# Making the low halves of a mixer's plain weight blocks on ScalarE and by an adding DMA

## The chip, the cores and the metric

The kernel runs on one core of one Trainium2 chip. The core has TensorE (PE: matrix products), VectorE (DVE), ScalarE (ACT), GpSimd (POOL, used here only to issue DMAs that add to their target) and SyncE (SP, which issues the plain DMAs). Each engine works through its own queue in order; semaphores carry the dependences between them. The metric is the device time of one execution in microseconds, less is better; the time given is the median of the runs.

## The reference

Two layers of a decoder trunk over 512 tokens of width 1024, in float32. Each layer is a half-weighted SwiGLU feed-forward block, a mixer, and a second feed-forward block, all with RMS norms around them:

```
h = rms_norm(x, gn[0])
x = x + 0.5 * rms_norm(swiglu(h, w_ffn1_gate[l], w_ffn1_up[l], w_ffn1_down[l]), gn[1])
h = rms_norm(x, gn[2])
proj = h @ w_in[l]
hq, hf, hi, hg, aq, ak, av, gate_a, gate_b = jnp.split(proj, IN_SPLITS, axis=-1)
y_hg = hgrn2_mixer(hq, hf, hi, hg, lb_all[l], hgrn_head_gain[l]) @ w_branch_hgrn[l]
y_at = swa_sink_attention(aq, ak, av, attn_sinks[l]) @ w_branch_attn[l]
mixed = jax.nn.sigmoid(gate_a) * y_hg + jax.nn.sigmoid(gate_b) * y_at
x = x + rms_norm(mixed @ w_out[l], gn[3])
```

`hgrn2_mixer` is a gated linear recurrence over 4 heads of 128 by 128 state; `swa_sink_attention` is attention with 8 query heads over a window of 128 tokens with a learned sink. A second feed-forward block, built like the first, ends the layer.

## The kernel before

**Products in two halves.** TensorE multiplies in a rounded float32 format (`F32R`). To keep float32 accuracy every operand is split into a high half, the operand rounded, and a low half, what the rounding left. `mm3` (a product helper) then makes three products: high with high, high with low, low with high. Nearly all of TensorE's work goes through `mm`, whose matmul is line 115; transposes are line 122.

**The weight stream.** All weights lie in one array, `wall`, of units of 128 by 1024 float32 (512 KB). The class `Stream` (the object `ws`) brings them in order through three rings of buffers: `W32` = 4 raw buffers (tag `w32`, filled by SP's loads of line 241), and `WS` = 6 buffers each for high (`whi`) and low (`wlo`) halves. `Stream.split` makes one unit ready: ScalarE casts the raw block to the high half (line 321), and the low half is made in one of two ways, by the kind of the item. For the kind "u" VectorE subtracts the high half from the raw block (line 328). For the kinds "v", "a" and "d" ScalarE multiplies the raw block by -1 into the low buffer (line 325), and POOL issues a DMA that adds the raw block to it (line 326). The multiply rounds, so raw minus rounded remains, as in the other way; it reads the raw block alone and does not wait for the cast. A raw buffer is given back when all that read it are done, and only then SP loads the unit four places on. Units are split three ahead of the one in use, as far as the six low and high buffers allow.

**What uses the stream.** A mixer's first 34 units are plain blocks: the projections of two recurrence heads (`quad`), attention's keys, queries and values (`project`), two projections by tokens (`project_tok`), two more heads, and the first gate columns with their branch weights (`branch`). After these come units of the fast matrix products (`gates`, items "a" to "d") and the rows of `w_out`.

**What sets the order.** TensorE's order is written out by hand. The recurrence, the attention and the end of each norm run as coroutines; `Order` counts a time from the matmuls issued and resumes each coroutine after a wait given in the table `WAIT`. The order on the other engines is chosen by a scheduler that knows priorities and an estimate of each step; where `pin` stands, the order of the program is kept.

**The start of a mixer.** The end of the preceding feed-forward block, in `down`, is laced into the mixer's start. `Pre.turn` transposes the normed tokens back (line 122) and ScalarE copies them, scaled by a gain, to the high halves (line 581) while VectorE makes the low halves (line 587). For the last tokens `post` and `norm` run this chain: VectorE adds two partial products (line 708), ScalarE squares with a running sum (line 596), VectorE and ScalarE make the root (lines 601 to 603), VectorE scales (lines 727 and 738), and TensorE transposes the result.

**The recurrence.** Each head's scores are built level by level: `meet` (lines 984 to 988) multiplies decays in on VectorE, ScalarE and VectorE fill a tile `mv` (lines 995 to 1000), TensorE multiplies it, and VectorE copies the product under a mask into place (line 972).

Of the kernel before, what the change touches and what calls it, by code (L numbers as in the profile page):

```python
# [23 lines left out]
H = 4  # L24
# [12 lines left out]
W32, WS, AHEAD, TAIL, PLAIN, FIRST, EARLY, LATE = 4, 6, 3, 4, 4, 7, 4, 8  # L37
# [8 lines left out]
def trunk(ctx: ExitStack, tc: tile.TileContext, xin, wall, gains, lbT, hgain, sinks, c_dist, c_mask, c_ident, out):  # L46
# [328 lines left out]
    ws = Stream()  # L375
# [894 lines left out]
    for l in range(DEPTH):  # L1270
        for n in (0, 2, 4):
            if n == 2:
                ws.plain(2 * H + 6 + 8 + LATE * 3 // 2)
                for _ in range(KT - LATE // 2):
                    ws.gates()
                ws.rows(KT, False)
            else:
                p = FIRST if l + n == 0 else PLAIN
                ws.plain(min(2 * p, 8))
                ws.plain(max(2 * p - 8, 0), "v")  # L1280
                ws.pairs(FT - p)
                ws.rows(FT, True)
# [151 lines left out]
```

## Time and profile before

| | |
|---|---|
| median of 3 runs | 2127.11 us (2126.46 to 2127.39) |
| span of the profiled execution | 2123.9 us |
| its own device time | not listed apart; the runs are 2.6 to 3.5 us above its span |
| TensorE busy | 2110.6 us, 99% of the span |
| VectorE busy | 1573.4 us, 74% |
| ScalarE busy | 1119.0 us, 53% |
| POOL busy | 152.2 us, 7% |
| granted TensorE clock | 0.999 |

In the rows of the profile, a group has the line, the engine, the operation, out<-in by the names of the tiles, the shape and the count; then the busy time in us, the mean time of one in ns, and the idle time of the engine just before them with what ended most of it. A row of the timeline has the start and the length in us, then the same names; a row of several instructions (x4) covers them from the first start to the last end. A row of the waits has who waited for whom, the total in us, the number and the longest. PEld is TensorE's loading of weights, which overlaps its products. The first mixer's plain blocks are used from about 358 to 610 us, the second's from about 1409 to 1660 us.

### The profile page before, as it was taken

To read this page: it belongs to the slowest core of one execution; us is meant where nothing else is said; L and a number is where in the kernel's file an instruction comes from. 1 tells how busy PE (TensorE), PEld (TensorE's weight loads), DVE (VectorE), ACT (ScalarE), POOL (GpSimd) and SP (SyncE) were. 2 spreads that over 40 slices of the span, in tenths; PEclk is the share of its full clock that TensorE was granted. 3 is DMA by queue.
4 is the path that set the end of the run, shared out by engine and by line. 5 is a ranking of instruction groups with operands and counts; after the bars stand their busy time and mean duration, and the time that the engine had idled before them with its cause. 6 is when DMAs were issued, how large, how long until landed. Compare 5 with 4: busy or idle time off the path is not lost.

```text
span 2123.9 us, 34765 instructions
## 1 busy us (share of the span) xinstructions
PE 2110.6 (99%) x13293; PEld 1898.1 (89%) x13293; DVE 1573.4 (74%) x2793; ACT 1119.0 (53%) x1884; POOL 152.2 (7%) x180
## 2 busy tenths in 40 slices
PE   9999999999999999999999999999999999999998
PEld 8899988887888999998899998898778989999987
DVE  5877886768776777789587778767687757777884
ACT  7555555346445555556455556453554545555562
POOL 0011000000000011110001110000000000111000
PEclk9999999999999999999999999999999999999999
DMA  8677663221236357774447775632122463677751
GB/s 251 149 185 182 167 181 118 92 67 64 66 100 208 120 125 176 182 197 123 153 113 177 183 183 141 197 119 80 60 70 60 124 194 110 149 180 182 185 158 51
DMA packets 146870, 298.48 MB, mean 141 GB/s; under 512 B 15664, under 2 KB 73488, under 8 KB 146704
## 3 DMA queue, kind: packets, MB, share of 16 engines
q1 hardware_dynamic: 121216, 228.31, 32.7%
q0 software_dynamic: 25344, 67.91, 18.6%
q8 instruction: 104, 1.70, 0.3%
q14 instruction: 62, 0.51, 0.1%
q10 hardware_dynamic: 144, 0.05, 0.0%
HBM read 213.58 MB, written 14.73 MB: 107 GB/s over the span
## 4 chain that ended last, share of the span: by engine, by line
PE 75%; DVE 7%; ACT 3%; issue 1%; DMA 1%; SPq 0%; ACTq 0%; DVEq 0%
PE acc L115 55%; PE aux L115 19%; DVE s L398 1%; PE aux L122 1%; ACT whi L321 1%; DVE wlo L283 1%; DMA w<-wall 1%; DVE wlo L328 1%; PE acc L122 1%; ACT s L397 1%; DVE tt L265 0%; DVE w L264 0%; DVE s L273 0%; DVE w L274 0%; ACT whi L278 0%
## 5 line engine op out<-in xcount | busy, mean ns | idle before, releaser
L115 PE MATMUL acc<-s,whi 128*128 128x256 f32 (+1 forms) x4968 | 1068.8, 312 | 0.7 <-DVE s L901 0.7
L115 PEld LDWEIGHTS acc<-s,whi 128*128 128x128 f32 x4968 | 810.1, 191 | 48.7 <-issue 3.7
L115 PE MATMUL acc<-s,wlo 128*128 128x256 f32 (+1 forms) x2484 | 770.2, 310 | 0.1
L115 PEld LDWEIGHTS acc<-s,wlo 128*128 128x128 f32 x2484 | 474.1, 191 | 26.0 <-DVE wlo L328 0.4
L321 ACT CAST whi<-w 128x1024 fp32r<-128x1024 f32 (+1 forms) x341 | 316.6, 947 | 242.0 <-PE aux L115 100.2
L115 PE MATMUL acc<-whi,s 128*128 128x512 f32 x1264 | 414.5, 394 | 0.0
L321 ACT CAST whi<-tt 128x1024 fp32r<-128x1024 f32 x154 | 161.4, 1048 | 337.7 <-DVE tt L315 199.5
L328 DVE TENSOR_TENSOR wlo<-w,whi 128x1024 fp32r<-128x1024 f32 (+1 forms) x181 | 218.5, 1216 | 135.3 <-ACT whi L321 131.6
L115 PEld LDWEIGHTS acc<-whi,s 128*128 128x128 f32 x1264 | 237.1, 188 | 55.7 <-issue 3.2
L328 DVE TENSOR_TENSOR wlo<-tt,whi 128x1024 fp32r<-128x1024 f32 x154 | 188.1, 1222 | 101.6 <-ACT whi L321 101.6
L326 POOL DMA_DIRECT2D wlo<-w x160 | 138.2, 865 | 1723.5 <-ACT wlo L325 1363.1
L115 PE MATMUL acc<-wlo,s 128*128 128x512 f32 x632 | 246.7, 390 | 1.2 <-DVE wlo L283 1.2
L115 PE MATMUL aux<-s,whi 128*128 128x256 f32 x1232 | 225.1, 283 | 0.0
L115 PE MATMUL aux<-whi,s 128*128 128x512 f32 x592 | 196.7, 390 | 0.0
L115 PEld LDWEIGHTS aux<-s,whi 128*128 128x128 f32 x1232 | 192.2, 192 | 0.0
L115 PE MATMUL aux<-s,wlo 128*128 128x256 f32 x616 | 174.3, 283 | 0.0
L115 PEld LDWEIGHTS acc<-wlo,s 128*128 128x128 f32 x632 | 118.8, 188 | 25.5 <-DVE wlo L283 2.4
L115 PEld LDWEIGHTS aux<-whi,s 128*128 128x128 f32 x592 | 111.2, 188 | 22.9
L325 ACT ACTIVATE wlo<-w 128x1024 fp32r<-128x1024 f32 (+1 forms) x160 | 129.8, 844 | 0.0
L397 ACT CAST s<-s 128x512 fp32r<-128x512 f32 (+1 forms) x164 | 88.4, 580 | 75.8 <-DVE s L456 72.2
L115 PEld LDWEIGHTS aux<-s,wlo 128*128 128x128 f32 x616 | 118.3, 192 | 0.0
L115 PE MATMUL aux<-wlo,s 128*128 128x512 f32 x296 | 115.2, 389 | 0.0
(182 smaller groups left out, 2189.1 us busy)
## 6 DMA issues: line engine op xcount, KB each, us to landing
w<-wall SPq DMA_DIRECT2D x267, 512.0 KB, 3.7
wlo<-w POOLq DMA_DIRECT2D x83, 512.0 KB, 5.5
w<-wall SPq DMA_DIRECT2D x288, 128.0 KB, 3.4
wlo<-w POOLq DMA_DIRECT2D x77, 256.0 KB, 3.3
x_d<-s SPq DMA_DIRECT2D x48, 256.0 KB, 2.1
s<-x_d SPq DMA_DIRECT2D x48, 256.0 KB, 5.5
w<-wall SPq DMA_DIRECT2D x34, 256.0 KB, 3.2
s<-wall SPq DMA_DIRECT2D x64, 128.0 KB, 3.7
```

The source lines that it names most:

```text
L115: nc.tensor.matmul(o, lhsT, rhs, start=start, stop=stop)
L122: nc.tensor.transpose(o, src, ident)
L283: nc.vector.tensor_tensor(it.lo[:, h[c]], w[c], it.hi[:, h[c]].bitcast(F32), op=ALU.subtract)
L321: i = nc.scalar.copy(it.hi[:, c], w[:, c])
L325: nc.scalar.mul(it.lo[:, c], w[:, c], -1.0)
L326: nc.gpsimd.dma_start(it.lo[:, c].bitcast(F32), w[:, c], accum_op=ALU.add)
L328: nc.vector.tensor_tensor(it.lo[:, c], w[:, c], it.hi[:, c].bitcast(F32), op=ALU.subtract)
L397: nc.scalar.copy(hi, src)
L398: nc.vector.tensor_tensor(lo, src, hi.bitcast(F32), op=ALU.subtract)
```

## The change

The 34 plain units of each mixer were one group of the kind "u". Now the first 4 stay of that kind, and the other 30 are of the kind "v". Their high halves are still cast by ScalarE; their low halves are made by ScalarE's multiply and POOL's adding DMA instead of VectorE's subtraction. Nothing else is edited; the order on VectorE and ScalarE around these steps is chosen anew by the scheduler, that on TensorE and SP stays as it was, instruction for instruction.

```
-                ws.plain(2 * H + 6 + 8 + LATE * 3 // 2)
+                ws.plain(4)
+                ws.plain(2 * H + 2 + 8 + LATE * 3 // 2, "v")
                 for _ in range(KT - LATE // 2):
                     ws.gates()
                 ws.rows(KT, False)
```

With `H` = 4 and `LATE` = 8 the old count is 34 and the new ones are 4 and 30.

## The prediction

> **What bounds the kernel now.** I read the page's busy shares first, then the chain that ended last, then the two mixer stretches as windows, then the waits.
>
> ```profile
> span 2123.9 us, 34765 instructions
> PE 2110.6 (99%) x13293; PEld 1898.1 (89%) x13293; DVE 1573.4 (74%) x2793; ACT 1119.0 (53%) x1884; POOL 152.2 (7%) x180
> PE 75%; DVE 7%; ACT 3%; issue 1%; DMA 1%; SPq 0%; ACTq 0%; DVEq 0%
> ...
> 358.00:610.00 252.00, 250.40 (x1397) 210.32 (x1396) 187.73 (x464) 121.95 (x254) 1.54 (x2) 1.00 0.23 74
> 1409.00:1660.00 251.00, 249.40 (x1393) 209.47 (x1392) 187.32 (x463) 120.95 (x252) 0.94 (x2) 1.00 0.23 73
> ...
> PE aux L115 <- DVE s L972: 3.2, 2, 1.6
> ```
>
> The windows' columns are length, then busy time and count of PE, PEld, DVE, ACT and POOL, the granted clock, the DMA share and GB/s. They are the stretches of the two mixers in which the 34 plain blocks of each are used. TensorE is busy for all but 1.60 us of either (252.00 - 250.40 and 251.00 - 249.40), at full clock, and the wait list gives that idle time an owner: one wait of 1.6 us in each mixer, for VectorE's L972. VectorE is busy for 74% of these stretches and ScalarE for 48%; neither bounds them. The order on TensorE is written out by hand and is the same in the changed kernel, so only two things can move the time: a stop of TensorE that goes, or a new one. All stops that the list shows here are worth 3.2 us, 0.15% of the time, which is the ceiling of a gain. About 0.2% (4.25 us) is what a measurement of this kernel can tell from no change.
>
> **The change, part by part.** For 30 blocks in each of two mixers VectorE's subtraction goes; a negating multiply on ScalarE and an adding DMA from POOL's queue come.
>
> ```profile
> L328 DVE TENSOR_TENSOR wlo<-w,whi 128x1024 fp32r<-128x1024 f32 x179 | 217.2, 1222 | 135.3 <-ACT whi L321 131.6 <-PE aux L115 1.6 <-DMA w<-wall 1.3
> L325 ACT ACTIVATE wlo<-w 128x1024 fp32r<-128x1024 f32 x83 | 86.8, 1046 | 0.0
> L326 POOL DMA_DIRECT2D wlo<-w x160: 862/862/1159, 29.6 to 1989.8; - x160
> DMA to landing us min/median/max: 3.2/4.6/7.5
> ```
>
> VectorE loses 60 x 1.222 = 73.3 us, ScalarE gains 60 x 1.046 = 62.8 us, POOL 60 x 0.862 = 51.7 us. The first mixer's stretch becomes 187.73 - 36.7 = 151.1 us of VectorE and 121.95 + 31.4 = 153.3 us of ScalarE out of 252. All of it lies beside TensorE, so what counts is place, not amount.
>
> *When a block is ready.* The subtraction ended 1.2 us after the cast; the new way takes 1.05 for the multiply, about 0.3 to POOL's start and 4.6 (3.2 to 7.5) to the landing, 6 us and at most 9. The first of the 30 has least room:
>
> ```profile
> 366.16 1.98 ACT L321 CAST whi<-w 128x1024 fp32r<-128x1024 f32 x2
> ...
> 383.70 0.39 PE L115 MATMUL acc<-s,wlo 128*128 128x512 f32 x1
> 395.04 0.39 PE L115 MATMUL acc<-s,wlo 128*128 128x512 f32 x1
> ```
>
> Cast from 366.16, low half read at 383.70: 16.5 us after the cast's end. Its multiply does not need the cast at all, and in the changed order stands well ahead of it. The third, cast at 374.67 (row below), is read at 395.04, 20 us later, and the lead grows from there. Nothing on the path, 0; without that cover it would be some 5 us a block.
>
> *When a raw buffer comes free.* The load four blocks on now waits for the landing instead of the subtraction. The tightest is that of the block cast at 374.67, whose buffer is loaded for the cast at 389.57:
>
> ```profile
> 374.67 1.05 ACT L321 CAST whi<-w 128x1024 fp32r<-128x1024 f32 x1 [3.60 <-PE acc L115]
> 389.57 1.04 ACT L321 CAST whi<-w 128x1024 fp32r<-128x1024 f32 x1 [2.80 <-PE acc L115]
> DMA to landing us min/median/max: 3.3/3.5/5.7
> ...
> 429.86 0.40 PE L115 MATMUL acc<-whi,s 128*128 128x512 f32 x1
> ```
>
> 374.67 + 1.05 + 1.05 + 0.3 + 4.6 + 3.5 = 385.2, before 389.57; with both maxima 390.3, 0.7 late, against a cast whose block TensorE first reads at 429.86. SP's order is unchanged; what queues behind the waiting load there is other loads. 0. POOL's queue holds nothing else in these stretches (two instructions in the first one). 0.
>
> *ScalarE's queue at the start of each mixer.* This is the step on the path. The changed order has the first two multiplies of a mixer (1.046 each, spaced 0.94, as the pair of casts above) between the second and the third scaled copy L581, before the down projection's last tokens are normalised. The rows of before:
>
> ```profile
> 356.85 1.56 ACT L581 ACTIVATE s<-acc,g_sb 128x256 fp32r<-128x256 f32 x4
> 358.29 0.85 ACT L581 ACTIVATE s<-aux,g_sb 128x256 fp32r<-128x256 f32 x2
> 359.00 0.66 ACT L596 ACTIVATE s<-s 128x512 f32<-128x512 f32 x1
> 359.61 0.66 ACT L596 ACTIVATE s<-s 128x512 f32<-128x512 f32 x1
> 360.13 0.23 ACT L596 ACTIVATION_READ_ACCUMULATOR s<-s 128x1 f32 x1
> 361.64 0.29 ACT L602 ACTIVATE rt<-ss,rt 128x1 f32<-128x1 f32 x1 [1.28 <-DVE rt L601]
> ...
> 359.24 0.68 DVE L708 TENSOR_TENSOR s<-aux,s 128x512 f32<-128x512 f32 x1
> 359.83 0.87 DVE L587 SCALAR_TENSOR_TENSOR s<-acc,g_sb,s 128x256 fp32r<-128x256 f32 x2
> 360.62 0.87 DVE L587 SCALAR_TENSOR_TENSOR s<-aux,g_sb,s 128x256 fp32r<-128x256 f32 x2
> 361.40 0.21 DVE L601 TENSOR_SCALAR rt<-ss 128x1 f32<-128x1 f32 x2
> 366.49 0.88 DVE L738 TENSOR_SCALAR s<-s,rt 128x512 f32<-128x512 f32 x2
> ...
> 326.54 11.25 SPq L241 DMA_DIRECT2D w<-wall  x3
> 358.42 0.40 PE L115 MATMUL acc<-s,whi 128*128 128x256 f32 x2
> 367.09 0.60 PE L122 MATMUL acc<-ident,s 128*128 128x128 f32 x4
> ```
>
> The third L581 goes from 357.57 to 359.45, and with it all behind it on ScalarE by 1.88: the last L581 ends at 361.02, the second square's sum is read out at 360.36 + 1.88 = 362.24. ScalarE had been idle for 1.28 before L602, because VectorE was still busy with L587; that idle time takes up most of it. L602 now starts at the sum, 362.25, instead of 361.64: +0.61. From L602 to L738 it is one chain of square, root and scaling, so L738's first half ends at 367.59 instead of 366.98 (second L738 starts 0.40 after the first; each takes 0.49). The second of the four transposes reads it, at 367.20 in before; at the L972 stop TensorE starts 0.14 after VectorE's end, so it starts at 367.73: 0.53 of new idle time in a mixer, 1.06 in both (the second mixer has the same rows around 1408). Bounds: 0, if the chain has more play than its rows show; 1.88 - 0.22 + 0.14 = 1.80 a mixer, 3.6 in all, if nothing is taken up (0.22 is from 366.98 to 367.20). I take 0.53, as the idle row of 1.28 is right there. The multiplies' own waits end in time: the loads that they need were issued by 337.8 (326.54 + 11.25), and TensorE gives back the low buffers with its last reads of the down projection, before it turns to the mixer at 358.42; the second multiply starts at 358.52.
>
> *The L972 stop.* VectorE and TensorE there:
>
> ```profile
> 397.05 1.23 DVE L328 TENSOR_TENSOR wlo<-w,whi 128x1024 fp32r<-128x1024 f32 x1 [2.42 <-ACT whi L321]
> 398.19 0.68 DVE L401 SCALAR_TENSOR_TENSOR s<-acc,s 128x512 fp32r<-128x512 f32 x1
> 400.60 1.29 DVE L972 COPY_PREDICATED s<-mask,aux 128x128 f32<-128x128 int32 x4
> 396.92 0.59 ACT L400 ACTIVATE s<-acc 128x512 fp32r<-128x512 f32 x1
> 401.74 0.89 PE L115 MATMUL aux<-mv,s 128*128 128x192 f32 x4 [1.60 <-DVE s L972]
> ```
>
> The subtraction at 397.05 goes, but L401 behind it needs ScalarE's L400, which ends at 397.51 and itself waits for TensorE. So L401 starts at 397.57, 0.62 earlier, not 1.2. The changed order puts one more masked copy ahead of the one that TensorE waits for, 0.28 by the spacing of the copies in the row of four. Gain 0.34 a mixer, 0.68 in both. Bounds: all of 3.2, or 0 if the reordering eats it.
>
> *ScalarE elsewhere.* At some ten places a mixer a multiply now stands directly ahead of a step that had followed at once, and pushes it by up to 0.95. The tightest one I find feeds TensorE thus:
>
> ```profile
> 569.19 1.05 ACT L321 CAST whi<-w 128x1024 fp32r<-128x1024 f32 x1 [0.78 <-PE acc L115]
> 570.28 0.59 ACT L1043 COPY s<-aux 128x512 f32<-128x512 f32 x1
> 571.47 1.72 PE L115 MATMUL aux<-s,s 128*128 128x128 f32 x14
> ```
>
> L1043 ended at 570.87 and its reader is the seventh of the fourteen records, 572.13; pushed by 0.8 it ends at 571.7, still in time. At the other places I find over a microsecond left. 0; if all ten were passed on in full, 9.5 us a mixer.
>
> **Sum.** +1.06 - 0.68 = +0.38 on a span of 2123.9: 2124.3. The span stands 3.2 below the median of the runs, 2127.11 (launch and end lie around it), so 2127.5.
>
> **Rivals.**
> - *The start passes on the whole push.* +3.6 - 0.68: 2130.0. For it: the chain from square to transpose has only 0.22 to spare. Against it: the 1.28 of idle time.
> - *ScalarE becomes what TensorE waits for* (slower). In-order ScalarE takes 60 more steps among copies and exponentials that TensorE reads within one or two microseconds. If half of the ten pushes of 0.95 in each mixer reach TensorE, 9.5 us: 2137. It decides from the point where such a step has under 0.95 left; only L1043 and the start come near in the rows.
> - *VectorE's relief reaches everything.* Both L972 stops go and the start is absorbed: 2127.1 - 3.2 = 2123.9, still short of 0.2%. Against it: L400 holds L401.
> - *POOL's work holds VectorE up.* If the 0.862 of POOL for each of the two first adds, issued around 359 to 361 among the L587, stopped VectorE, that would be 1.72 a mixer on the thin chain, 3.4 in all: 2130.9. Against it: POOL's 862/862/1159 over 160 adds, beside a VectorE that is busy 74% of the time, leaves little sign of one waiting for the other. [...]
> - *The change doesn't do what it says*: excluded, the built order has 60 more multiplies and adds and 60 fewer subtractions, in the mixers alone.
>
> **Chances.** The forecast and its small neighbours (2125.5 to 2129.5) 0.66; whole push 0.10; relief 0.08; POOL 0.05; ScalarE 0.11. Slower by over 0.2% is the ScalarE case and a little of the push and of POOL: 0.14. Faster by over 0.2% needs more idle time than the windows show: 0.04. Within: 0.82. The range, 2123.7 to 2132.0, holds all but the ScalarE case and takes in the bounds of the start and of the L972 stop.
>
> **What would show it.** In the profile after: L325 over whole blocks x143 at 1046 and L328 over raw blocks x119; in the two stretches VectorE near 151 and ScalarE near 153; a new wait of TensorE (L122) for VectorE's L738 of about half a microsecond in each mixer; the wait for L972 at 2.5 instead of 3.2. Waits of TensorE for ScalarE's L1043, L1182 or L1210, or for a low half whose add is late, would make it wrong on the slow side; a list without the L972 waits on the fast side.

## The result, and the profile after

The changed kernel takes 2129.83 us (2128.28 to 2131.07, 20 runs), the kernel before 2127.11 (2126.29 to 2128.21, 20 runs): 1.0012 times the time before, 95% interval 1.0007 to 1.0018. That is 2.7 us slower, within the 0.2% that was called no change and inside the range, but well off the forecast of 2127.5. The profiled execution took 2129.19 us with a span of 2127.4; the span is 3.5 us above that of before.

The page after, its busy times:

```profile
span 2127.4 us, 34931 instructions
PE 2111.7 (99%) x13293; PEld 1897.8 (89%) x13293; DVE 1509.2 (71%) x2733; ACT 1174.7 (55%) x1944; POOL 203.9 (10%) x240
```

VectorE has lost 64.2 us, ScalarE gained 55.7, POOL 51.7. The groups by form show the edit itself:

```profile
L325 ACT ACTIVATE wlo<-w 128x1024 fp32r<-128x1024 f32 x143 | 150.1, 1051 | 7.1 <-PE acc L115 7.1
...
L328 DVE TENSOR_TENSOR wlo<-w,whi 128x1024 fp32r<-128x1024 f32 x119 | 144.1, 1222 | 108.8 <-ACT whi L321 105.7 <-PE aux L115 2.1 <-DMA w<-wall 0.8
```

The two mixers as windows, with the columns as before (length, then PE, PEld, DVE, ACT, POOL, the granted clock, DMA share, GB/s); the second is taken 2 us later than before, because the kernel is behind by then:

```profile
358.00:610.00 252.00, 250.40 (x1396) 210.11 (x1395) 155.43 (x433) 149.67 (x284) 27.34 (x32) 1.00 0.56 136
1411.00:1662.00 251.00, 249.42 (x1392) 209.29 (x1391) 155.11 (x433) 148.65 (x283) 26.76 (x31) 1.00 0.56 136
```

TensorE is busy in these stretches for as long as before (250.40 and 249.42 us, against 250.40 and 249.40), although DMA traffic has nearly doubled (from 74 to 136 GB/s). The mixers did not lose the 2.7 us. The list of TensorE's waits says where it went:

```profile
PE aux L115 <- DVE s L972: 2.5, 2, 1.3
PE aux L115 <- DMA wlo<-w: 1.9, 1, 1.9
...
PE acc L122 <- DVE s L738: 0.6, 2, 0.3
```

The first and the last row are the two steps that the prediction named. The middle one is new and was not foreseen: the list has one wait of TensorE, in the whole kernel, for a low half that an adding DMA makes. It stands neither in a mixer nor on a block that the change touches. It is the last half block (an item "d") of layer 0's second feed-forward. Laid matmul by matmul beside the trace before, TensorE falls behind by 0.55 us at 366, regains 0.33 at 400, falls behind by 2.17 at 943 (times of before), and then by 0.53 and back by 0.34 in the second mixer.

The rows of before and after around that stop, from the timelines. Before:

```profile
939.25 0.86 POOL L326 DMA_DIRECT2D wlo<-w  x1 [8.39 <-DVE m L879]
...
944.17 0.28 PE L115 MATMUL aux<-s,wlo 128*128 128x256 f32 x1
```

After:

```profile
938.87 0.63 ACT L325 ACTIVATE wlo<-w 128x512 fp32r<-128x512 f32 x1
...
941.75 0.86 POOL L326 DMA_DIRECT2D wlo<-w  x1 [10.35 <-ACT s L397]
...
946.48 0.39 PE L115 MATMUL aux<-s,wlo 128*128 128x256 f32 x1 [1.92 <-DMA wlo<-w]
```

ScalarE's multiply ended at 938.87 + 0.63 = 939.50, and POOL's queue had been empty for 10.35 us. Yet the add began at 941.75, 2.25 us behind the last thing that it depends on (the release named in the row, L397, is only the nearest event in time). The usual lag, the median over all adds of this trace, is 0.29. Then its landing took 4.7 us, where the same half block before took 3.6:

```profile
w<-wall SPq DMA_DIRECT2D x6, 128.0 KB, 2.8
wlo<-w POOLq DMA_DIRECT2D x1, 256.0 KB, 4.7
```

This is the list of DMA issues from 941 to 947. 941.75 + 4.7 = 946.45, and TensorE goes on at 946.48. Six loads of 128 KB were issued in the same time as the late add. Their number alone does not tell the two kernels apart, for in the kernel before, from 939 to 945, there are more:

```profile
w<-wall SPq DMA_DIRECT2D x9, 128.0 KB, 3.2
wlo<-w POOLq DMA_DIRECT2D x1, 256.0 KB, 3.6
```

What differs is where they stand: after, four loads were issued between 0.84 us before the add's start and 0.48 us behind it; before, none was issued from 1.5 us before its start to 1.1 us behind it.

Going through all adds of both traces for their lag behind the last dependence gives four late ones after and three before, always 53 adds apart, alternately 0.8 to 1.0 and 2.25 us late: the 61st, 114th, 167th and 220th. Before, the 114th add stood at 1235.32, in layer 1's first feed-forward. Its multiply, the first of the two in the upper row, ended at 1233.07, 2.25 us earlier:

```profile
1232.44 1.57 ACT L325 ACTIVATE wlo<-w 128x512 fp32r<-128x512 f32 x2
...
1235.32 1.75 POOL L326 DMA_DIRECT2D wlo<-w  x2 [10.35 <-ACT s L861]
```

It landed 3.26 us after its start, TensorE read it 3.56 us after its start and did not stop. The mixer of layer 0 now issues 30 adds more, so the 114th add comes much sooner: it is that last half block.

So my theory for the runs: the mixers cost +0.2 us each, as predicted, and some 2 us come from a late add that every 53rd suffers, and that the 30 new adds have shifted to a place without room. The rivals: the new traffic disturbs landings; or ScalarE's added work delays something there. Under both, the stop would follow the mixers' change and not the count of adds.

### The profile page after: what moved, and what is told of

The parts are those of the page before. It is cut to its first block, busy times and chain, and to the rows that moved or that the text cites. A ratio compares the mean times of both kernels' runs of the same rounds, so it can differ in the third digit from the quotient of the medians.

```text
span 2127.4 us, 34931 instructions
## 1 busy us (share of the span) xinstructions
PE 2111.7 (99%) x13293; PEld 1897.8 (89%) x13293; DVE 1509.2 (71%) x2733; ACT 1174.7 (55%) x1944; POOL 203.9 (10%) x240
## 5 line engine op out<-in xcount | busy, mean ns | idle before, releaser
L326 POOL DMA_DIRECT2D wlo<-w x220 | 189.9, 864 | 1674.4 <-ACT wlo L325 1268.7
L328 DVE TENSOR_TENSOR wlo<-tt,whi 128x1024 fp32r<-128x1024 f32 x154 | 188.1, 1222 | 102.4 <-ACT whi L321 102.2
L328 DVE TENSOR_TENSOR wlo<-w,whi 128x1024 fp32r<-128x1024 f32 (+1 forms) x121 | 145.4, 1213 | 108.8 <-ACT whi L321 105.7
L325 ACT ACTIVATE wlo<-w 128x1024 fp32r<-128x1024 f32 x220 | 193.1, 902 | 7.1 <-PE acc L115 7.1
L397 ACT CAST s<-s 128x512 fp32r<-128x512 f32 (+1 forms) x164 | 88.2, 580 | 71.3 <-DVE s L456 67.7
```

What stands on the lines that cost most here:

```text
L325: nc.scalar.mul(it.lo[:, c], w[:, c], -1.0)
L326: nc.gpsimd.dma_start(it.lo[:, c].bitcast(F32), w[:, c], accum_op=ALU.add)
L328: nc.vector.tensor_tensor(it.lo[:, c], w[:, c], it.hi[:, c].bitcast(F32), op=ALU.subtract)
L397: nc.scalar.copy(hi, src)
```

## The experiments

The kernels ran on several chips, and the kernel before ran on each of them. Its median there lies between 2126.19 and 2127.11 us, so each kernel is set against the kernel before on its own chip.

**29 blocks instead of 30: one add fewer ahead of the place.**

```
                 ws.plain(4)
-                ws.plain(2 * H + 2 + 8 + LATE * 3 // 2, "v")
+                ws.plain(2 * H + 1 + 8 + LATE * 3 // 2, "v")
+                ws.plain(1)
```

> 29 of the 34 plain blocks of each mixer by the adding DMA instead of 30: the last block goes back to VectorE, the start of the mixer is as in the changed kernel. Count theory (every 53rd adding DMA of POOL's queue starts late, every second time by 2.25 us, and the 114th one happened to fall on the last half block of layer 0's second feed-forward): the 114th add is now the first L409 add near 972, which has 13.6 us of room, so TensorE's stop of 1.92 us at 946 goes, while the mixers keep +0.53 (L738) and -0.34 (L972) each: span about 2125.2, time about 2127.6, 2.2 below the changed kernel. The 220th add falls on a half block with 5.5 - 2.25 = 3.3 us of room, which may cost up to 0.5. Rival, landing times disturbed by the traffic of the many adds: the stop for wlo near 946 stays, 2129.8. Rival, ScalarE's extra multiplies cost the 2 us: 2129.7, as 58 of 60 are still there.

Measured 2127.56 us against 2126.22 before, 1.0005 (0.9996 to 1.0014). The late add stands where it was expected, on the first L409, and the stop at 946 is gone:

```profile
975.54 0.86 POOL L409 DMA_DIRECT2D s<-s  x1 [34.19 <-ACT whi L278]
```

The time meets the expected 2127.6 by luck, because the kernel before is faster on this chip (2126.22 against 2127.11): it is 1.3 us above it, where 0.5 was expected. The mixers' two rows are the changed kernel's. The 220th add and the one queued behind it make the matmuls 0.46 and 0.53 us later at 1944 and 1947 (times of before), 1.0 in all where up to 0.5 was allowed for, and another 0.64 is lost near 958 (left open below):

```profile
PE aux L115 <- DVE s L972: 2.5, 2, 1.3
...
PE acc L122 <- DVE s L738: 0.6, 2, 0.3
...
PE acc L115 <- DMA wlo<-w: 0.3, 1, 0.3
PE aux L115 <- DMA wlo<-w: 0.2, 1, 0.2
```

**28 blocks, beginning two later: no multiply among the L581.**

```
-                ws.plain(4)
-                ws.plain(2 * H + 2 + 8 + LATE * 3 // 2, "v")
+                ws.plain(6)
+                ws.plain(2 * H + 8 + LATE * 3 // 2, "v")
```

> 28 of the 34: the first six plain blocks of each mixer instead of four stay with VectorE, so that no multiply stands between the L581 of the mixer's start. My theory: the stop for L738 (0.6 us in each mixer) goes, the L972 stop stays at 2.5 in sum, and the 114th add is the second L409 add (11.8 us of room), so no stop at 946: span 2123.9 - 0.7 = 2123.2 to 2123.5, time about 2126.5, 0.6 below the kernel before. The 220th add, on a half block with 5.4 - 2.25 = 3.2 us of room, may cost up to 0.6. If the start is pushed whoever the first block is (the multiplies merely move), the L738 stop stays and the time is about 2127.6. Rival, traffic: the stop at 946 stays, 2128.6.

Measured 2126.48 against 2126.22, 1.0000 (0.9991 to 1.0009). In the trace L738 is gone from TensorE's waits, L972 is at 2.5, no wait for wlo is listed, and ScalarE's chain stands as before the change, with its idle time back:

```profile
358.34 0.85 ACT L581 ACTIVATE s<-aux,g_sb 128x256 fp32r<-128x256 f32 x2
...
361.69 0.29 ACT L602 ACTIVATE rt<-ss,rt 128x1 f32<-128x1 f32 x1 [1.28 <-DVE rt L601]
```

So the start's push comes from the first two multiplies alone and can be avoided. The mixers do give their 0.66 us, but the kernel is not 0.6 faster: its matmuls end 0.6 later than those of before, by 0.59 at the first load (4 to 7 us) and by 0.85 near 958, where the first products after the feed-forward wait for casts, and these casts for loads. The first of these comes and goes with the run, since kernels that differ in nothing there have it or not. The second is left open below.

**The kernel before with 30 small adds ahead of everything.** This asks whether the count alone makes the stop.

```
     nc.vector.memset(eps_t, EPS)
+    spare = const([16, 30, 8], "spare")
+    nc.vector.memset(spare, 0.0)
+    for k in range(30):
+        nc.gpsimd.dma_start(spare[:, k, :], ones[:16, :8], accum_op=ALU.add)
```

> The kernel before, with 30 small adding DMAs (16 partitions x 8 numbers into a tile that nothing reads) at the very start of POOL's queue, while that queue is empty up to 29 us; no mixer is changed. Count theory, by adding DMA: the 114th add is now the last half block of layer 0's second feed-forward, it starts near 941.5 instead of 939.25 and TensorE stops for wlo near 944 for 1.5 to 2.2 us; the late one at 1235 is gone: time about 2129.2, as slow as the changed kernel without one edit of its mixers. If the period counts bytes or descriptors, 30 adds of this size are worth only some four whole ones or less: the late add moves a few places within layer 1's first feed-forward, where it has 5.6 - 2.25 = 3.4 us of room, and the time stays 2127.1. If the lateness at 941 belongs to the mixers' change, 2127.1 too, with no late add at 941.

Measured 2125.22 against 2126.22, 0.9996 (0.9987 to 1.0005); no late add near 941 and no stop. The expectation fell, but not to "nothing moves": the late adds now were the 55th, 108th and 161st of the kernel's own (6 places earlier, 0.8 to 1.2 us late) and the 99th (15 places earlier, 1.55). So it is not the number of adds alone that counts; a small add counts less.

**The changed kernel with two adds of 128 partitions at the start.** The same lines with `const([P, 2, 8], "spare")`, `range(2)` and `ones[:, :8]`, in the changed kernel.

> The changed kernel, with two small adding DMAs (128 partitions x 8 numbers into a tile that nothing reads) at the very start of POOL's queue. Count theory: the late add is the one two places earlier, the last but one half block of layer 0's second feed-forward: it starts near 931.8 instead of 929.58, and the stop for wlo, 1.5 to 2 us, stands near 936 instead of 946; the time stays 2129.8. Any theory in which the place belongs to that block or to the traffic around it leaves the stop at 946; one in which it is chance from run to run leaves no stop, or one anywhere.

The place came out to the row: exactly two adds earlier, the half block at 929 in the changed kernel, is now 2.25 us late, and the last one is punctual.

```profile
931.14 1.75 POOL L330 DMA_DIRECT2D wlo<-w  x2 [10.35 <-ACT s L865]
939.38 0.86 POOL L330 DMA_DIRECT2D wlo<-w  x1 [6.49 <-DMA w<-wall]
```

The size did not. The wait is 0.3 us, the matmuls fall behind by 0.74 there, and the time is 2126.30 against 2126.22, 1.0000 (0.9991 to 1.0009). The reason is in the DMA issues of 930.5 to 937:

```profile
wlo<-w POOLq DMA_DIRECT2D x1, 512.0 KB, 5.7
w<-wall SPq DMA_DIRECT2D x4, 128.0 KB, 4.2
wlo<-w POOLq DMA_DIRECT2D x1, 256.0 KB, 3.2
```

Here the late half block landed in 3.2 us. Being late costs 1.4 us less (0.74 against 2.17 by the matmuls) where the landing is not slow as well.

**The kernel before with 30 adds of 128 partitions.** The same lines with `const([P, 30, 2], "spare")` and `ones[:, :2]`; no mixer is changed.

> The kernel before, no mixer changed, with 30 adding DMAs of 128 partitions x 2 numbers (into a tile that nothing reads) at the start of POOL's queue. The run with 30 adds of 16 partitions moved the late starts by only 6 and 15 places, the run with two of 128 partitions by exactly 2; so I now hold that the period goes by the partitions (descriptors) of an add. Then 30 of 128 partitions count in full: the late start of 2.25 us falls on the last half block of layer 0's second feed-forward, 941.5 instead of 939.25, lands beside the 128 KB loads of the mixer after it, and TensorE stops for wlo near 944 for about 2 us; the time is 2 us above the kernel before. If bytes count, 30 adds of 1 KB count for nothing, the late start stays at 1235 and the time is that of before. If the stop belongs to the change in the mixers, likewise that of before, with no stop at 944.

Measured 2127.80 against 2126.19, 1.0009 (1.0000 to 1.0017). The stop of the changed kernel stands in the kernel before:

```profile
940.84 0.86 POOL L330 DMA_DIRECT2D wlo<-w  x1 [10.35 <-ACT s L401]
```

```profile
PE aux L115 <- DVE s L976: 3.2, 2, 1.6
...
PE aux L115 <- DMA wlo<-w: 1.3, 1, 1.3
```

The first fence is POOL's timeline, the second the waits (lines are 4 higher here; L976 is L972). TensorE falls behind by 1.58 us at 943, 1.6 us in the time. Neither ScalarE's multiplies nor the traffic in the mixers is there. The 30 adds together move 30 KB, so bytes do not count either.

**The changed kernel with 50 such adds.**

> The changed kernel with 50 such adds (128 partitions x 2 numbers) at the start of POOL's queue. By partitions counted, the late starts fall on adds that have room: 2.25 us on the mixers' adds near 530 and 1485 (35 us and more of room), 0.7 on the 11th add and on one L409. No stop for wlo at 946, none of 2 us elsewhere; L738 and L972 as in the changed kernel. Time 2.2 us below the changed kernel of the same call, within 0.5 of the kernel before. If the stop at 946 comes of the traffic or of ScalarE's extra work, it stays and the time is the changed kernel's.

Measured 2135.76 against 2126.19, 1.0045 (1.0033 to 1.0058): far off, and the fault is the probe's. The 50 adds fill POOL's queue, so that the first real add starts at 42.80 instead of 29.65, and TensorE stopped:

```profile
PE aux L122 <- ACT s L524: 7.5, 1, 7.5
```

The matmuls are 10.76 us behind by 58, and 10.32 at the end: after this stop the kernel loses nothing against the kernel before. The 2.25 us late adds fell on mixer blocks (541.94 and 1495.71), there is no wait for wlo, and the mixers show +0.53 and +0.55, -0.33 and -0.34. The time itself tells nothing.

**The changed kernel again**, on the chip of the two kernels above and of the one below:

> The changed kernel itself, on the chip of the other runs of this call. The late add at 941.7 and the stop of about 1.9 us for wlo near 946 repeat if they are set by the program; if the lateness is chance, it is elsewhere or gone. About 2.5 us above the kernel before (2.0 of it the stop, 0.4 the mixers).

2128.59 against 2126.19, 1.0012 (1.0003 to 1.0021). The late adds are the 61st, 114th, 167th and 220th again, with the same lags to 0.01 us, and the stop is 1.6 us:

```profile
PE aux L115 <- DVE s L972: 2.5, 2, 1.3
PE aux L115 <- DMA wlo<-w: 1.6, 1, 1.6
```

**Only the first two blocks of the 30.**

```
                 ws.plain(4)
-                ws.plain(2 * H + 2 + 8 + LATE * 3 // 2, "v")
+                ws.plain(2, "v")
+                ws.plain(2 * H + 8 + LATE * 3 // 2)
```

> Only the first two of the 30 blocks of each mixer by the adding DMA, the other 28 back on VectorE. The two multiplies stand between the L581 as in the changed kernel. By my step, the stop for L738 is there (0.5 us of shift in each mixer) and the L972 stop is as in the kernel before, 3.2 in sum: +1.06 in all from the mixers. If the push came from the whole load of 30 multiplies on ScalarE, there is no L738 stop. The 2.25 us late add falls on a half block of layer 1's first feed-forward near 1193 with 6.0 - 2.25 = 3.7 us of room, no stop or up to 0.3. Time about 1.1 above the kernel before.

2127.30 against 2126.19, 1.0006 (0.9997 to 1.0014). The L972 stop is at its old size and the L738 stop is there, for two multiplies alone:

```profile
PE aux L115 <- DVE s L972: 3.2, 2, 1.6
...
PE acc L122 <- DVE s L738: 0.3, 1, 0.3
```

The list shows the stop in the first mixer only. Matmul by matmul it is 0.54 there and, in two pieces (0.22 at 1410, 0.30 at 1418), 0.52 in the second: 1.06 expected, 1.06 found. The late add stood at 1224.88, and the add pushed behind it cost 0.2; 1193 was miscounted, since two adds more in layer 0 move it by two places only.

**The change in one layer alone.** `"v"` becomes `"v" if l == 0 else "u"`, and then `"v" if l else "u"`.

> The change in layer 0's mixer alone, 30 blocks; layer 1's mixer is as before. My theory: mixer +0.53 - 0.34 near 366 and 400, the late add still falls on the last half block near 941.7 and stops TensorE for about 1.6 to 1.9 us near 946, nothing in layer 1: 2.0 to 2.2 us above the kernel before. If ScalarE's extra work or the added traffic costs the time, both layers pay alike and this kernel pays half of the changed kernel's 2.4 to 2.7: about 1.3 above.

> The change in layer 1's mixer alone; layer 0's is as before. My theory: the 114th add is again the one near 1235 with room for 2.25 us, no stop for wlo near 944; mixer 1 gives +0.53 - 0.34: 0.2 us above the kernel before. If ScalarE's extra work or the traffic costs the time: about 1.3 above.

With layer 0 alone 2128.78 against 2126.35, 1.0012 (1.0003 to 1.0021): 2.4 us, as much as the changed kernel lost (2.7 and 2.4). With layer 1 alone 2126.75, 1.0001 (0.9992 to 1.0010): 0.4 us. The waits with layer 0 alone (the row of L727 is in the kernel before too, at the same size):

```profile
PE aux L115 <- DVE s L972: 2.9, 2, 1.6
PE acc L122 <- DVE s L727: 2.9, 1, 2.9
PE aux L115 <- DMA wlo<-w: 1.6, 1, 1.6
```

and POOL's queue with layer 1 alone, where the 114th add is back in its old place, late and harmless:

```profile
1235.72 1.75 POOL L326 DMA_DIRECT2D wlo<-w  x2 [10.36 <-ACT s L861]
```

The intervals of the times are about 2 us wide in all and would not settle this by themselves. The traces do: at the matmuls of the mixers the two kernels show +0.54 -0.33 and +0.53 -0.34, each in its own mixer, and only the first has +1.82 at 943. A cost that goes with the multiplies, or with the traffic, would have been shared by both.

**30 adds of 64 partitions in the kernel before**, to see what the period counts:

> The kernel before with 30 adding DMAs of 64 partitions x 2 numbers at the start of POOL's queue. It asks what the period counts. 30 adds of 128 partitions moved the late starts by 30 places, 30 of 16 partitions by 6 (the starts late by about 0.7) and by 15 (the part that makes every second one later still). If each counts a fixed part and a part in proportion to the partitions, 64 of them move the two by 30 x 0.54 = 16 and 30 x 0.71 = 21 places: late adds at the 45th, 98th and 151st, and one at the 93rd. If it counts adds above some size alone, 6 and 15, or 30 and 30. The time: as before.

The late adds were the 45th, 98th and 151st, 16 places earlier, as worked out. The separate one at the 93rd did not appear; instead the 98th was 2.42 us late. A single run took 2125.98, against 2126.35 for the kernel before.

## Why the prediction was right or wrong, point by point

- *The ceiling and the bound.* Right: TensorE stays at 99% and the changes in time that are traced here are stops of TensorE that came or went.
- *ScalarE's queue at the start of each mixer, +0.53 each.* Right in place, mechanism and size. After the change:

```profile
357.58 2.00 ACT L325 ACTIVATE wlo<-w 128x1024 fp32r<-128x1024 f32 x2
359.48 0.84 ACT L581 ACTIVATE s<-acc,g_sb 128x256 fp32r<-128x256 f32 x2
...
362.30 0.29 ACT L602 ACTIVATE rt<-ss,rt 128x1 f32<-128x1 f32 x1
...
367.15 0.88 DVE L738 TENSOR_SCALAR s<-s,rt 128x512 f32<-128x512 f32 x2
...
367.69 0.55 PE L122 MATMUL acc<-ident,s 128*128 128x128 f32 x3 [0.33 <-DVE s L738]
```

  L602 at 362.30 (predicted 362.25), the transposes at 367.69 (367.73), the idle time of 1.28 before L602 used up. The two-block run shows that these two multiplies do it alone, the 28-block run that without them it is gone.
- *The L972 stop, -0.34 each.* Right: 2.5 instead of 3.2 in sum, -0.33 and -0.34 by the matmuls, in every mixer that has the later blocks and in none that has not.
- *The engines' busy time.* In the first mixer's stretch VectorE is at 155.4 and ScalarE at 149.7, not 151 and 153: over the kernel each subtraction took 64.2 / 60 = 1.07 us of busy time with it and each multiply brought 55.7 / 60 = 0.93, since the records of neighbours overlap (by 0.09 us between the subtraction at 397.05 and L401 before, by 0.10 between the multiplies at 357.58 and L581 after); the means of one, 1.22 and 1.05, count that overlap twice.
- *When a block is ready, the raw buffers, ScalarE elsewhere: 0.* Right in the mixers, where TensorE is as busy as before. The landing was sized too small: 4.6 us is the median over whole and half blocks, with 7.5 as the longest, and the whole blocks of the first mixer took 4.5 to 9.0 us, 4.8 in the median. The room there covered it. The tightest place, L1043, ran 0.47 us ahead of its reader.
- *"POOL's queue holds nothing else in these stretches ... 0."* This is the step that failed. It looked for what the new adds would queue behind and for what queues behind them, in the mixers. It did not ask whether an add depends on how many went before it. In POOL's queue of the trace before, three adds start 0.8, 2.25 and 0.8 us late with nothing ahead of them, 53 adds apart; the one with 2.25 had 3.56 us to its reader and stopped nobody. 30 adds more in layer 0 move that lateness onto an add that TensorE needs 4.9 us after its start, beside a burst of loads: a term of +1.6 to +2.2 us, against 0. Part of its price stood in the rows of before: the add would start 2.25 - 0.29 = 1.96 us later, and between its landing and its reader there were 4.92 - 3.56 = 1.36 us, so the lateness alone gives a stop of about 0.6 us, as an estimate. The other parts could not be read there: the landing took 1.1 us more, and the multiply before the add ended 0.3 us later against TensorE.
- *The sum.* +0.38 was forecast; +0.4 of the mixers was found, and +1.6 to +2.2 of the late add: 2.0 to 2.6, against 2.7 and 2.4 in the times of the changed kernel (2.72 and 2.40). With layer 0 alone it is +0.2 and +1.8 against 2.43. The rest is below what the traces repeat. That 2129.83 fell inside the range is luck: the range was wide enough for the bounds of two other steps, and the term that came was not in it. The time alone would even have pointed to a wrong rival, the whole push with its 2130.0, which the trace excludes, since the push was 0.53. One term of the sum was misread without harm to the difference, the 3.2 us between span and time, put down there to launch and end: no run here shows what lies in them, and in every other execution of these kernels the time is 1.73 to 1.87 us above the span, so the trace of before is of an execution of about 2125.7 us, a fast one; that is why the two spans differ by 3.5 us and the medians by 2.7.
- *The rivals.* The whole push, the full relief and ScalarE as the bound did not come. POOL's work does not hold VectorE up: with 32 and 31 adds in the two stretches, the two forms of L587 take 476 and 475 ns over the whole kernel after, 476 and 476 before, the longest of the 80 is 484 in both, and L328 takes 1222 in both.
- *What would make it wrong.* "A low half whose add is late" was named as a sign on the slow side, and that is what came, but it was looked for among the 30 blocks and stood outside of them.

**What stays open.** Near 958, where TensorE enters the attached products after the feed-forward, the changed kernel lost 0.24 and 0.74 us in two runs, the 29 blocks 0.64 and the 28 blocks 0.85, but the changed kernels with small adds ahead and the one with layer 0 alone nothing (-0.21 to 0). In the 28 blocks it goes back to a cast that waited 0.6 us longer. Whether this is chance of the loads there or belongs to some of the orders is not settled. Why the last half block of layer 0's second feed-forward lands in 3.6 us in some kernels and in 4.4 to 4.7 in others is not shown by an experiment. In all thirteen traces it goes with the loads beside it: in the five with a slow landing, three or four loads of 128 KB were issued between 1.2 us before the add's start and 0.5 us behind it; in the other eight none was issued from 1.4 us before to 1.1 us behind. One of the five (the changed kernel with two adds) has this add punctual, so lateness is not needed for a slow landing.

**A version that beats both** was not found. 28 blocks beginning at the seventh is the best form of the change by its trace: it has neither the start's push nor the stop, since the late add falls on an L409. In time it equals the kernel before (1.0000); the changed kernel's ratio was 1.0012 both times, and the intervals overlap.

## What to carry to other kernels

When an edit adds instructions to a queue, ask of every later instruction in that queue whether its lateness depends on how many went before it: walk the whole queue of the trace for starts that come late with nothing ahead of them, note their period, and see where the edit puts them. An effect that appears outside of the edited stretch, on code that is the same, need not be chance; adding work that nothing reads, sized so that it shifts only the count, tells it apart from the edit in one run. Put such probes where the queue has room, or they cost more than they show.

## What the runs showed of the hardware

Adding DMAs issued by POOL start late with a period: in the kernels without added small transfers every 53rd, alternately 0.8 to 1.0 us and 2.25 us behind their last dependence, where 0.29 is usual, with the same places and lags in two traces of the changed kernel. An add that follows the one of 2.25 us closely is late with it: it starts 0.59 us after it and 1.90 us behind its own multiply, in all eight traces that have such a pair at 2.25. The period does not go by bytes: an add of 128 x 2 or 128 x 8 numbers counts like one of 128 x 512 or 128 x 1024. It goes by partitions: 30 adds of 128, 64 and 16 partitions move the late starts by 30, 16 and 6 places.

What a smaller add counts can be estimated from these places alone: 30 adds of 16 partitions moved the late starts by 6 and 30 of 128 by 30, so that one of 16 counts 0.2 and one of 128 counts 1. On a straight line between the two, as the last expectation worked out, one of 64 counts 0.54 and 30 of them 16.3; the run's 16 agrees, as places are whole numbers. In proportion to the partitions, with no fixed part, 30 of 16 would count 30 x 16/128 = 3.75, the "some four" of one expectation, against the 6 found. Two expectations name descriptors as what may be counted; no run here shows that, nor what POOL does while an add is late. The further lateness of every second one (the 1.3 to 1.5 us that make 2.25 of it) moved by 15 places with 30 adds of 16 partitions, and by 16 with 64, and follows no count that I have.
